# Copying chunk operands to a slot of their own, weighting the head sum in its selector, and keeping a state sum and a gated result in PSUM: a two-layer RWKV-7 and attention kernel

## The chip, the cores and the metric

The kernel runs on one core of a Trainium2 chip. The metric is the device time of one execution in microseconds (us). Before the change it took 797.93 us, the median of three runs (796.20, 797.93, 800.12). The engines are named as the profile names them: PE is the matmul engine and PEld its weight loads, DVE the vector engine, ACT the scalar engine, POOL the third elementwise engine, SP the engine that issues most DMAs. SBUF is the on-chip memory that holds tiles; PSUM is the memory that PE writes to, in 8 banks.

## The reference

The input `x` has 512 tokens of 1024 features. Layer 0 is an RWKV-7 time mixing: four dense projections `r, k, v, g` of the token-shifted input, per-channel decays, and for each of 16 heads of 64 channels a recurrence over the tokens; its output is normalised per head, a bonus is added, and it is gated and projected. Layer 1 is a differential attention. Each layer ends with a per-layer embedding. The lines that the change touches in the kernel compute these:

```python
def step(state, inp):
    r_t, w_t, k_t, v_t, kk_t, a_t = inp
    s_kk = jnp.einsum('bhij,bhj->bhi', state, kk_t)
    state = (state * w_t[:, :, None, :]
             - s_kk[..., None] * (kk_t * a_t)[:, :, None, :]
             + v_t[..., None] * k_t[:, :, None, :])
    return state, jnp.einsum('bhij,bhj->bhi', state, r_t)
...
y = ((y - mean) * lax.rsqrt(var + GN_EPS) * lnx_g.astype(f32).reshape(H, N)
     + lnx_b.astype(f32).reshape(H, N))
y = y + jnp.sum(r * k * r_k.astype(f32), axis=-1, keepdims=True) * v
y = y.reshape(B, S, D).astype(xn.dtype) * jax.nn.silu(g)
return y @ w_out
```

All is float32, with a dense product done as three matmuls of rounded high and low parts (`mm3`, L285 to L287).

## The kernel before

**Staging.** Features lie on the 128 partitions in 8 tiles, tokens along the free axis. From about 85 us the dense projections run, two halves of 512 output features each (half 0 and half 1, `g` in the code below). As the halves of `r, k, v` come out, layer 0 is worked in 8 chunks of 64 tokens for each half: `gram` (L984) builds the products of a chunk pair `cq`; `inverse` (L1013 on), four in all, two for each half, solves the triangular systems of four chunks by 31 substitution steps on DVE (L1051, L1054), then two sets of small matmuls (L1087, L1101), and copies the results back with small copies of 32 x 128 (L270 is the helper `copy`, used with many tiles; L1115). `operands` transposes each chunk's `BK` tile on PE (L1149), `recur` carries the 64 x 64 states of 8 heads through the chunks, and `finish` normalises, adds the bonus, gates, transposes and splits the result in a high and a low part for the output projection. POOL clears tiles (L1144, L1212) and does parts of the finish. Half 0's recurrence lies at about 162 to 243 us, half 1's at 305 to 379; dense matmuls of the other half, of `p` and `g`, and then of the output projection fill PE between the steps.

**One chunk of the recurrence.** Products of the chunk (L1188) and the state's part (L1201) sum up in a bank `pA`; part of it is copied to `gt` (an H tile cleared by POOL at L1212), products with `gt` are added, and a part is copied to `uv`. L1229 multiplies the transposed operands with `uv` into a bank `pS`; DVE adds this to the state (L1241, SBUF plus PSUM, written to SBUF) and multiplies with the chunk's decay `pcall` (L1244, SBUF to SBUF), which the next chunk's L1201 waits for. ACT copies the output to `yT` (L1249).

**What sets the order.** The order of all instructions on each engine, and of the DMAs on SP, is fixed when the program is written: a planner, `Streams`, runs the stages as coroutines. A `yield` of an engine and a cost asks for the next instructions; `wait` and `set` are events; `take` and `free` count buffers: `R` (43 tiles of 128 x 1024), `H` (9 of 128 x 512), PSUM banks (`pw`, `pd`). The planner takes the step that could start first by its own clocks and costs; a `+` behind an engine's name also takes a port that its DVE and POOL steps share, a `!` lets a stage's next step start without waiting for this one; a choice such as `ACT/DVE+` goes to the engine that would be done first. So changed costs, waits or buffers move instructions far from the lines that are edited. On the chip each engine works its own list in order and waits for semaphores.

**Names.** `hsel` is a selector of 128 x 32 that sums the channels of each head on PE (L824); `rkvec` holds the weights `r_k`; `rk` the products r times k. `BK` holds keys by token and feature, `vcD`, `gD`, `mD`, `peD` lie in DRAM, `in_eye` is an input with a unit matrix; L1030 copies it from an H tile to the bank in which DVE substitutes. L1501 copies a product of the `p` embedding out of PSUM. L749 and L750 belong to the decays' small projections, L1456 and L1414 to the output of the layers, and L521 and L525 to the mixing of the input.

Of the kernel before, what the change touches and what calls it, by code (L numbers as in the profile page):

```python
# [8 lines left out]
F32 = mybir.dt.float32  # L9
F32R = mybir.dt.float32r  # L10
AF = mybir.ActivationFunctionType
ALU = mybir.AluOpType
# [190 lines left out]
def yoco_kernel(ctx: ExitStack, tc: tile.TileContext, I, out):  # L203
# [489 lines left out]
    hsel = later("hsel", [P, 32])  # L693
    rkvec = later("rkvec", [P, NT])
    der = T(ax, [P, 6, NT], "der")
    omm = T(ax, [P, 4, NT], "omm")
# [117 lines left out]
    SQ, CK = {}, {}  # L814

    def head_sums(g, what):

# [5 lines left out]
        for q in range(4):  # L823
            nc.tensor.matmul(pn[32 * q : 32 * q + 32], hsel, SQ[what, 4 * g + q], start=True, stop=True)  # L824
        yield "free", "H", 4
# [31 lines left out]
    def k_evac(i, pk):  # L857
# [44 lines left out]
        nc.gpsimd.tensor_mul(v4(rk), part_r(i), K)  # L902
        yield "ACT", 0.57
        nc.scalar.activation(rk, rk, AF.Copy, scale=rkvec[:, i : i + 1])
        yield "set", ("rk", i)
# [15 lines left out]
    sc.add(x_scale(), XLP[0])  # L921
    sc.add(late_loads(), 1)
    for g in range(2):
        sc.add(lora2(g), LO2P[g])
# [196 lines left out]

    def bkt(i, cq, par):
        return BK[i][:, cq, 2 * par : 2 * par + 2, :].rearrange("p a j -> p (a j)")

    def operands(g):
# [4 lines left out]
        for c_ in range(NC):  # L1130
# [4 lines left out]
            if par == 0:  # L1135
                yield "take", "R", 1
                UV[cq, g] = R([P, 2, S])
            t = UV[cq, g][:, par]
# [9 lines left out]
            for ii in range(4):  # L1148
                nc.tensor.transpose(pt[:, ii * P : (ii + 1) * P], bkt(4 * g + ii, cq, par), ident)  # L1149
            yield "ACT", 0.63  # L1150
            for ii in range(4):
                nc.scalar.copy(bkt(4 * g + ii, cq, par), pt[:, ii * P : (ii + 1) * P])
            yield "free", "pw", 1
# [4 lines left out]
    def recur(g):  # L1158
# [14 lines left out]
        for c_ in range(NC):  # L1173
# [49 lines left out]
            if c_ < NC - 1:  # L1223
                yield "take", "pw", 1
                pS = bank("pw")
                yield "PE", 0.55
                for ii, hh in heads:
                    hs = slice(hh * HN, hh * HN + HN)
                    nc.tensor.matmul(  # L1229
                        pS[hs, cols(ii, hh)], bkt(4 * g + ii, cq, par)[:, hs], uv[:, cols(ii, hh)], start=True, stop=True  # L1230
                    )
                pv = pS.rearrange("p (a b) -> p a b", b=P)
            yield "PE!", 0.55
            products(pA, 1, ROFF, uv, False)
            if c_ < NC - 1:
                for hh in range(2):
                    hs = slice(hh * HN, hh * HN + HN)
                    sv, qv = S_[hs, :, hs], pv[hs, :, hs]
                    if c_ > 0:
                        yield "DVE!", 0.42  # L1240
                        nc.vector.tensor_add(sv, sv, qv)  # L1241
                        qv = sv
                    yield "DVE+!", 0.42
                    nc.vector.tensor_mul(sv, qv, bc(pcall[hs, c_, 4 * g : 4 * g + 4].unsqueeze(2), [HN, 4, HN]))  # L1244
# [6 lines left out]
            if par == 1:  # L1251
                yield "free", "R", 3
            yield "set", ("rec", c_, g)
# [3 lines left out]
    def finish(cq, g):  # L1257
# [60 lines left out]
        ENG[sc.eng].tensor_sub(lo, w, hi.bitcast(F32))  # L1318
        yield "free", "R", 1
# [664 lines left out]
```

## Time and profile before

| what | value |
|---|---|
| median of three runs | 797.93 us (796.20 to 800.12) |
| profiled execution | 797.09 us, span 795.3 us |
| PE busy | 756.1 us, 95% |
| DVE busy | 589.8 us, 74% |
| ACT busy | 454.5 us, 57% |
| POOL busy | 201.9 us, 25% |
| mean granted clock of PE | 0.989 |
| HBM read, written | 110.13 MB, 37.75 MB |

The span is the time from the first to the last instruction that the profiler saw; the rest of the execution's time lies around it. In the rows of a view of groups there stand the line, the engine and the operation, the tile written and the tile read, shape and count, then busy time and the mean of one in ns, and the idle time of the engine just ahead of them with what ended it. A row of waits gives total, times and longest. A row of a timeline or of the chain begins with its start and duration.

### The profile page before, as it was taken

How to read it: one execution, taken by the hardware profiler on the slowest of the kernel's cores; microseconds unless marked ns; L12 is line 12 of the kernel's file. 1: busy time of each engine (PE TensorE's matmuls, PEld its weight loads, DVE VectorE, ACT ScalarE, POOL GpSimd, SP SyncE). 2: the span in 40 equal slices, each digit the busy share in tenths (PEclk: the TensorE clock that was granted, in tenths of full speed). 3: DMA queues.
4: the chain of work that ended last, by engine and by line, in shares of the span. 5: the costliest groups of instructions: out<-in, count | busy, mean ns of one | idle time of the engine just before them, and what ended most of it. 6: DMA issues, size and time to landing. Idle time of an engine off the chain costs nothing.

```text
span 795.3 us, 13941 instructions
## 1 busy us (share of the span) xinstructions
PE 756.1 (95%) x5016; PEld 605.1 (76%) x5016; DVE 589.8 (74%) x1360; ACT 454.5 (57%) x1078; POOL 201.9 (25%) x221
## 2 busy tenths in 40 slices
PE   6899999998999899999989999999999999999996
PEld 3576578875777677777778888887888888888884
DVE  2989999976798898998676685446874768835844
ACT  3779745688875446664444564333764566743431
POOL 2416615521451425666010010000000001100000
PEclk9999999998999899999999999999999999999998
DMA  8585669843684687463446444488943523314602
GB/s 325 197 285 196 245 225 290 298 147 105 209 286 171 217 301 258 145 228 105 133 166 247 133 146 135 172 309 226 312 158 92 159 53 121 117 43 159 259 6 106
DMA packets 66677, 148.79 MB, mean 187 GB/s; under 512 B 6576, under 2 KB 27312, under 8 KB 66608
## 3 DMA queue, kind: packets, MB, share of 16 engines
q1 hardware_dynamic: 43824, 112.25, 41.9%
q10 hardware_dynamic: 22784, 35.66, 13.1%
q8 instruction: 39, 0.64, 0.3%
q14 instruction: 30, 0.25, 0.1%
HBM read 110.13 MB, written 37.75 MB: 186 GB/s over the span
## 4 chain that ended last, share of the span: by engine, by line
PE 70%; DVE 8%; ACT 8%; DMA 8%; issue 2%; POOL 2%; SPq 1%; ACTq 0%; POOLq 0%; DVEq 0%
PE p L285 18%; PE p L287 18%; PE p L286 18%; PE p L1788 2%; PE p L984 2%; PE p L1188 2%; ACT R L270 1%; PE p L1753 1%; PE p L1752 1%; PE p L1201 1%; DMA R<-bD 1%; PE p L1779 1%; DMA RAW<-in_ple_w 1%; PE p L1410 1%; DMA R<-mD 1%
## 5 line engine op out<-in xcount | busy, mean ns | idle before, releaser
L285 PE MATMUL p<-R,R 128*128 128x512 f32 x800 | 326.4, 408 | 3.2 <-DVE R L270 1.7
L286 PE MATMUL p<-R,R 128*128 128x512 f32 x800 | 314.1, 393 | 3.8 <-DVE R L525 3.6
L287 PE MATMUL p<-R,R 128*128 128x512 f32 x800 | 314.4, 393 | 0.0
L285 PEld LDWEIGHTS p<-R,R 128*128 128x128 f32 x800 | 151.3, 189 | 37.1 <-DVE R L270 1.9
L287 PEld LDWEIGHTS p<-R,R 128*128 128x128 f32 x800 | 151.0, 189 | 33.2 <-DVE R L1318 0.4
L286 PEld LDWEIGHTS p<-R,R 128*128 128x128 f32 x800 | 151.5, 189 | 32.4 <-DVE R L525 4.9
L318 POOL TENSOR_TENSOR R<-RAW,R 128x512 fp32r<-128x512 f32 x59 | 78.6, 1339 | 163.3 <-ACT R L270 89.1
L270 ACT CAST R<-RAW 128x512 fp32r<-128x512 f32 x110 | 66.1, 619 | 26.7 <-DMA RAW<-in_w_g 10.0
L318 DVE TENSOR_TENSOR R<-RAW,R 128x512 fp32r<-128x512 f32 x81 | 56.8, 715 | 11.0 <-ACT R L270 10.2
L324 DVE SCALAR_TENSOR_TENSOR R<-RAW,vec,R 128x512 fp32r<-128x512 f32 x64 | 46.6, 748 | 13.9 <-ACT R L322 13.7
L322 ACT ACTIVATE R<-RAW,vec 128x512 fp32r<-128x512 f32 x64 | 44.6, 720 | 17.0 <-DMA RAW<-in_b_w_in 9.1
L1397 POOL TENSOR_TENSOR hr<-hm,half 128x1 f32<-128x1 f32 x16 | 10.4, 648 | 147.2 <-DVE hm L1395 147.2
L1757 DVE CUSTOM_DVE_ANT_0 p<-p,cmask 128x128 f32<-128x128 f32 (+3 forms) x64 | 30.3, 509 | 17.4 <-PE p L1753 17.3
L1764 ACT ACTIVATE H<-p,mx 128x128 f32<-128x128 f32 (+3 forms) x64 | 33.3, 526 | 15.7 <-DVE mx L1761 14.1
L281 POOL TENSOR_TENSOR orr<-orm,half 128x4 f32<-128x4 f32 x8 | 8.4, 1055 | 123.3 <-DVE orm L279 93.3
L1054 DVE TENSOR_TENSOR p<-p,H 128x126 f32<-128x126 f32 (+22 forms) x124 | 32.6, 263 | 4.3
L1051 DVE TENSOR_TENSOR H<-p,R 128x126 f32<-128x126 f32 (+22 forms) x124 | 30.5, 246 | 1.1
L1534 DVE SCALAR_TENSOR_TENSOR R<-H,R 128x512 f32<-128x512 f32 x16 | 11.1, 691 | 24.5 <-ACT H L1527 23.1
L1527 ACT ACTIVATE H<-p 128x512 f32<-128x512 f32 x16 | 9.5, 596 | 31.6 <-PE p L287 31.6
L521 DVE SCALAR_TENSOR_TENSOR p<-R,vec,p 128x511 f32<-128x511 f32 x32 | 23.5, 747 | 5.4 <-ACT p L519 5.3
L519 ACT ACTIVATE p<-R,omm 128x512 f32<-128x512 f32 x32 | 22.0, 695 | 5.0 <-DVE R L525 3.7
L1788 PEld LDWEIGHTS p<-R,H 128*128 128x128 f32 x160 | 22.1, 191 | 2.8 <-ACT H L1805 0.5
(227 smaller groups left out, 1249.4 us busy)
## 6 DMA issues: line engine op xcount, KB each, us to landing
R<-mD SPq DMA_DIRECT2D x40, 512.0 KB, 5.3
mD<-R ACTq DMA_DIRECT2D x32, 512.0 KB, 4.3
RAW<-in_ple_gate SPq DMA_DIRECT2D x16, 512.0 KB, 3.7
RAW<-in_kv_w SPq DMA_DIRECT2D x16, 512.0 KB, 3.9
RAW<-in_b_w_in SPq DMA_DIRECT2D x16, 512.0 KB, 3.9
R<-bD ACTq DMA_DIRECT2D x24, 256.0 KB, 5.2
R<-in_x SPq DMA_DIRECT2D x8, 512.0 KB, 6.8
RAW<-in_w_r SPq DMA_DIRECT2D x8, 512.0 KB, 4.0
```

The lines of the kernel that those rows point to most:

```text
L270: (nc.scalar.copy if sc.eng == "ACT" else ENG[sc.eng].tensor_copy)(dst, src)
L285: nc.tensor.matmul(ps, ah, bh, start=first, stop=False)
L286: nc.tensor.matmul(ps, ah, bl, start=False, stop=False)
L287: nc.tensor.matmul(ps, al, bh, start=False, stop=last)
L318: ENG[sc.eng].tensor_sub(lo, f, hi.bitcast(F32))
L322: nc.scalar.activation(hi, f, AF.Copy, scale=g)
L324: nc.vector.scalar_tensor_tensor(lo, f, g, hi.bitcast(F32), ALU.mult, ALU.subtract)
L1051: ve.tensor_mul(tmp[:, 0:m, 0:w], bc(xs[:, s_ : s_ + 1, 0:w], [P, m, w]), bc(nb[:, s_ + 1 : 32, s_ : s_ + 1], [P, m, w]))
L1054: ve.tensor_add(xs[:, s_ + 1 : 32, 0:w], xs[:, s_ + 1 : 32, 0:w], tmp[:, 0:m, 0:w])
L1757: nc.vector.tensor_tensor_reduce(scs[m][:, 0:n], scs[m][:, 0:n], cmask[:, S - n : S], 1.0, -3.0e38, ALU.add, ALU.max, mx[:, m : m + 1])
L1764: nc.scalar.activation(E[m][:, 0:n], scs[m][:, 0:n], AF.Exp, bias=mx[:, m : m + 1], scale=0.125, accum_out=sm[:, m : m + 1])
L1788: nc.tensor.matmul(po[:, x * P : (x + 1) * P], aT[:, kb * P : (kb + 1) * P], vT[hg, kb // 2][:, kb % 2, x * P : (x + 1) * P], start=(kb == 0),
```

## The change

Four edits:

1. **Bonus.** The weights `r_k` are multiplied once into a set of eight selectors `hselr` (one DVE multiply of 128 x 8 x 32, after the first dense half of `r` is out), and the head sum of `rk` uses these. The scaling of each `rk` tile on ACT (L904, eight of 128 x 512) is gone.
2. **Operands.** The four transposes of a chunk were copied from their bank back into the `BK` tiles by four ACT copies of 128 x 128 (L1152); now one ACT copy of 128 x 512 writes them to a new `R` tile `BT`, shared by the chunk pair, from which the state product L1229 reads. A chunk pair takes two `R` tiles where it took one, and frees four where it freed three.
3. **State.** The sum of state and product is written back into the bank (`qv`), and the multiply with the decay reads it from there; the multiply no longer takes the planner's shared port.
4. **Finish.** The gated result (`scalar_tensor_tensor`, L1310) is written back into its bank; ACT always copies the high part from there, DVE always subtracts for the low part, and the bank is freed behind both. Before, the result went to the SBUF tile `w`, the bank was freed at once, and the planner chose ACT or DVE for the copy, POOL or DVE for the subtraction.

```diff
+    hselr = T(ax, [P, NT, 32], "hselr")
...
+    def bonus_maps():
+
+        yield "wait", ("r", 0)
+        yield "DVE+", 0.4
+        nc.vector.tensor_mul(hselr, bc(hsel.unsqueeze(1), [P, NT, 32]), bc(rkvec.unsqueeze(2), [P, NT, 32]))
+
...
-            nc.tensor.matmul(pn[32 * q : 32 * q + 32], hsel, SQ[what, 4 * g + q], start=True, stop=True)
+            sel = hsel if what == "sq" else hselr[:, 4 * g + q, :]
+            nc.tensor.matmul(pn[32 * q : 32 * q + 32], sel, SQ[what, 4 * g + q], start=True, stop=True)
...
-        yield "ACT", 0.57
-        nc.scalar.activation(rk, rk, AF.Copy, scale=rkvec[:, i : i + 1])
...
+    sc.add(bonus_maps(), 5)
...
             if par == 0:
-                yield "take", "R", 1
-                UV[cq, g] = R([P, 2, S])
+                yield "take", "R", 2
+                UV[cq, g], BT[cq, g] = R([P, 2, S]), R([P, 2, S])
...
-            yield "ACT", 0.63
-            for ii in range(4):
-                nc.scalar.copy(bkt(4 * g + ii, cq, par), pt[:, ii * P : (ii + 1) * P])
+                bk = BK[4 * g + ii][:, cq, 2 * par : 2 * par + 2, :].rearrange("p a j -> p (a j)")
+                nc.tensor.transpose(pt[:, ii * P : (ii + 1) * P], bk, ident)
+            yield "ACT", 0.5
+            nc.scalar.copy(BT[cq, g][:, par], pt)
...
-                        pS[hs, cols(ii, hh)], bkt(4 * g + ii, cq, par)[:, hs], uv[:, cols(ii, hh)], start=True, stop=True
+                        pS[hs, cols(ii, hh)], BT[cq, g][:, par, cols(ii, hh)], uv[:, cols(ii, hh)], start=True, stop=True
...
                         yield "DVE!", 0.42
-                        nc.vector.tensor_add(sv, sv, qv)
-                        qv = sv
-                    yield "DVE+!", 0.42
+                        nc.vector.tensor_add(qv, qv, sv)
+                    yield "DVE!", 0.42
                     nc.vector.tensor_mul(sv, qv, bc(pcall[hs, c_, 4 * g : 4 * g + 4].unsqueeze(2), [HN, 4, HN]))
...
-                yield "free", "R", 3
+                yield "free", "R", 4
...
-            nc.vector.scalar_tensor_tensor(w[:, xs], pt[:, xs], vcol(V_LB, 4 * g + x), gt[:, xs], ALU.add, ALU.mult)
-        yield "free", "pw", 1
+            nc.vector.scalar_tensor_tensor(pt[:, xs], pt[:, xs], vcol(V_LB, 4 * g + x), gt[:, xs], ALU.add, ALU.mult)
...
-        yield "ACT/DVE+", (0.52, 0.34)
-        copy(hi, w)
-        yield "Pool+/DVE+", (1.23, 0.6)
-        ENG[sc.eng].tensor_sub(lo, w, hi.bitcast(F32))
+        yield "ACT", 0.48
+        nc.scalar.copy(hi, pt)
+        yield "DVE", 0.6
+        nc.vector.tensor_sub(lo, pt, hi.bitcast(F32))
+        yield "free", "pw", 1
```

Lines of the changed kernel stand 5 to 9 below those of the kernel before: L1115 is L1122 there, L1030 is L1037, L1501 is L1506, L1249 is L1254, L1212 is L1218, L1144 is L1150, L1272, L1274, L1288, L1291 and L1293 are L1277, L1279, L1293, L1296 and L1298.

The planner makes a new order of it. On ACT, at the copies of the second inverse (half 0, 180 to 190 us before), the list was

```order
L1249 COPY R_1732<-p_1829 64x2x128 x2
L780 ACTIVATE H_1863<-p_1939,der_96 128x512
L270 COPY R_1064<-H_1849 32x2x2x32 x4
L270 COPY R_1065<-H_1849 32x2x2x32 x3
L270 COPY R_1205<-H_1849 32x2x2x32 x2
L270 COPY R_1206<-H_1849 32x2x2x32 x2
L1115 COPY R_1064<-p_1987 32x2x2x32
L1115 COPY R_1064<-p_1988 32x2x2x32
L1115 COPY R_1065<-p_1987 32x2x2x32
L1115 COPY R_1065<-p_1988 32x2x2x32
L1115 COPY R_1205<-p_1987 32x2x2x32
```

and is now

```order
L880 COPY H_1978<-p_1470 128x512
L1254 COPY R_1721<-p_1817 64x2x128 x2
L270 COPY R_1063<-H_1838 32x2x2x32 x4
L270 COPY R_1064<-H_1838 32x2x2x32 x4
L270 COPY R_1204<-H_1838 32x2x2x32 x3
L270 COPY H_2020<-p_1989 64x2x128 x2
L270 COPY R_1204<-H_1838 32x2x2x32
L270 COPY R_1205<-H_1838 32x2x2x32 x2
L1122 COPY R_1063<-p_1932 32x2x2x32
L1122 COPY R_1063<-p_1933 32x2x2x32
L1122 COPY R_1064<-p_1932 32x2x2x32
```

The two copies to `gt` (`H_2020`) of a chunk of the recurrence now stand among the inverse's copies to `G` (11 before and 14 now from ACT, then eight L1115 or L1122), and an activation of the decays (L780) no longer stands ahead of them.

On ACT around the copy of `in_eye` for the first inverse of half 1 (258 to 266 us before), the list was

```order
L1501 COPY H_2970<-p_2935 128x512
L1501 COPY H_2983<-p_2969 128x512
L1030 COPY p_3010<-H_2994 128x512
L270 COPY H_2993<-R_2877 32x128 x3
L270 COPY H_2993<-R_2878 32x128 x3
L1501 COPY H_3005<-p_2982 128x512
L1501 COPY H_3042<-p_3004 128x512
```

and is now

```order
L1506 COPY H_2915<-p_2870 128x512
L1506 COPY H_2933<-p_2914 128x512
L1506 COPY H_2961<-p_2932 128x512
L1037 COPY p_2996<-H_2983 128x512
L270 COPY H_2982<-R_2860 32x128 x4
L270 COPY H_2982<-R_2861 32x128 x4
L1506 COPY H_2975<-p_2960 128x512
```

One copy of the `p` embedding behind L1037 remains where two stood behind L1030, and eight small copies of the inverse where six were.

On POOL in the recurrence of half 1 (355 to 375 us before), the end of the list was

```order
L1144 MEMSET R_4250 64x2x128 x2
L1212 MEMSET H_4270 128x512
L1272 TENSOR_TENSOR R_4251<-R_4251,vmean_92 128x512
L281 TENSOR_TENSOR grsr_4240<-grsm_4239,half_90 128x8
L1288 TENSOR_TENSOR R_3485<-R_3485,grsr_4240 128x512
L1144 MEMSET R_4250 64x2x128 x2
L1274 TENSOR_TENSOR R_4251<-R_4251,bon_100 128x512
L1212 MEMSET H_4390 128x512
```

and is now

```order
L1218 MEMSET H_4112 128x512
L1150 MEMSET R_4093 64x2x128 x2
L1277 TENSOR_TENSOR R_4095<-R_4095,vmean_92 128x512
L281 TENSOR_TENSOR grsr_4137<-grsm_4136,half_90 128x8
L1279 TENSOR_TENSOR R_4095<-R_4095,bon_101 128x512
L1296 TENSOR_TENSOR R_3476<-R_3476,R_1704 128x512
L1298 TENSOR_TENSOR R_3476<-R_3476,R_3868 128x512
L1150 MEMSET R_4093 64x2x128 x2
L1218 MEMSET H_4254 128x512
```

Between two clearings of `gt` POOL has five steps of the finish where it had four, beside the operands' memsets. On PE the same recurrence now has 3 to 6 dense matmuls between a chunk's steps, where 9 to 21 stood, and its last product stands 48 dense matmuls earlier; 84 dense matmuls now follow the last finish's transposes before their result is first used, where the use followed at once.

More of the change, by code (lines that the diff above doesn't have):

```diff
@@ L1120, in inverse @@
         yield "set", ("prep", g, cp)
-    def bkt(i, cq, par):
-        return BK[i][:, cq, 2 * par : 2 * par + 2, :].rearrange("p a j -> p (a j)")
+    BT = {}
     def operands(g):
@@ L1148, in operands @@
             for ii in range(4):
-                nc.tensor.transpose(pt[:, ii * P : (ii + 1) * P], bkt(4 * g + ii, cq, par), ident)
-            yield "ACT", 0.63
-            for ii in range(4):
-                nc.scalar.copy(bkt(4 * g + ii, cq, par), pt[:, ii * P : (ii + 1) * P])
+                bk = BK[4 * g + ii][:, cq, 2 * par : 2 * par + 2, :].rearrange("p a j -> p (a j)")
+                nc.tensor.transpose(pt[:, ii * P : (ii + 1) * P], bk, ident)
+            yield "ACT", 0.5
+            nc.scalar.copy(BT[cq, g][:, par], pt)
             yield "free", "pw", 1
```

## The prediction, before the result was known

> **What bounds the kernel now.** I read the page first: the span and the busy time of each engine.
>
> ```profile
> span 795.3 us, 13941 instructions
> PE 756.1 (95%) x5016; PEld 605.1 (76%) x5016; DVE 589.8 (74%) x1360; ACT 454.5 (57%) x1078; POOL 201.9 (25%) x221
> ```
>
> PE is busy for 756.1 of 795.3 us, so a change that takes no matmul away, as this one, can win at most the 39.2 us in which PE stands still, and what PE runs below full clock. The edits lie between about 85 and 400 us. So I next read PE's waits, grouped by who ended them (us in total, times, longest):
>
> ```profile
> PE p L984 <- ACT H L1501: 3.1, 1, 3.1
> PE p L749 <- ACT R L1115: 1.8, 1, 1.8
> PE p L285 <- DVE R L270: 1.7, 1, 1.7
> PE p L1201 <- DVE R L1244: 1.6, 2, 0.8
> PE p L285 <- DVE R L800: 1.4, 1, 1.4
> ```
>
> These five rows, 9.6 us, are what the change can reach; the longer waits of that list belong to the start and the end of the program. Then the stretches, 20 us each (columns: PE, weight loads, DVE, ACT, POOL busy, granted clock, DMA share, GB/s), and two of 10 us:
>
> ```profile
> 180.00:200.00 20.00, 16.36 (x174) 11.93 (x167) 13.01 (x26) 16.19 (x44) 3.86 (x6) 0.83 0.36 122
> 200.00:220.00 20.00, 19.22 (x191) 15.36 (x189) 15.18 (x30) 17.67 (x41) 9.75 (x12) 1.00 0.54 188
> 220.00:240.00 20.00, 19.17 (x246) 15.07 (x245) 19.05 (x36) 13.13 (x33) 10.83 (x15) 1.00 0.88 305
> 340.00:360.00 20.00, 19.16 (x180) 15.37 (x179) 19.10 (x33) 12.28 (x32) 14.08 (x15) 1.00 0.68 224
> 360.00:380.00 20.00, 19.32 (x214) 14.90 (x213) 16.55 (x35) 8.91 (x23) 11.16 (x11) 1.00 0.34 100
> 185.00:195.00 10.00, 7.68 (x64) 5.84 (x65) 6.76 (x12) 9.46 (x23) 2.46 (x2) 0.66 0.14 44
> 262.00:272.00 10.00, 6.88 (x30) 5.34 (x29) 7.80 (x22) 7.61 (x20) 3.76 (x3) 0.66 0.40 136
> ```
>
> Two places stand out. At 185 to 195 ACT is full (9.46 of 10) while PE has 7.68, and the clock is 0.66: 0.34 x 10 = 3.4 us of full speed lost beside the waits. The same loss stands at 262 to 272. Everywhere else from 200 to 380 PE is over 19 of 20 busy, which leaves about 0.8 us per stretch.
>
> **The change part by part.** *Work that goes.* The groups by line:
>
> ```profile
> L904 ACT ACTIVATE H<-H,rkvec 128x512 f32<-128x512 f32 x8 | 5.8, 722 | 0.0
> L1152 ACT COPY R<-p 128x128 f32<-128x128 f32 x64 | 12.2, 278 | 1.9 <-PE p L1149 1.8
> L1456 ACT COPY R<-p 128x512 f32<-128x512 f32 x16 | 9.4, 587 | 24.6 <-PE p L287 24.4
> L1244 DVE TENSOR_TENSOR R<-R,pcall x24: 407/422/1280, 177.6 to 372.0; 64x256 f32<-64x256 f32 x24
> L1244 DVE TENSOR_TENSOR R<-p,pcall x4: 389/422/427, 166.8 to 308.4; 64x256 f32<-64x256 f32 x4
> L1318 DVE TENSOR_TENSOR R<-R,R 128x512 fp32r<-128x512 f32 x8 | 6.4, 796 | 0.4 <-ACT R L270 0.2
> L525 DVE TENSOR_TENSOR R<-p,R 128x512 fp32r<-128x512 f32 x32 | 21.4, 682 | 0.9 <-ACT R L523 0.5
> L521 DVE SCALAR_TENSOR_TENSOR p<-R,vec,p 128x511 f32<-128x511 f32 x32 | 23.5, 747 | 5.4 <-ACT p L519 5.3
> ```
>
> The bonus edit takes 8 scalings off ACT, 5.8 us, and adds one DVE multiply of 128x256 (under 0.69, L525's time for twice the width). The operands' 64 copies, 12.2 us, become 16 of the form of L1456, 9.4: 2.8 us less. Of the eight `hi` copies of the finish, those that DVE did now go to ACT, three at 0.587: 1.8 us more. ACT: 5.8 + 2.8 - 1.8 = 6.8 us less.
>
> On DVE the 24 state multiplies that read two SBUF tiles have a median of 422 ns but up to 1280; the four that read PSUM end at 427. If the tail goes, 15.2 us (24 x 0.633) becomes 24 x 0.422 = 10.1. The `lo` subtraction falls from 796 to L525's 682, 0.9 us for eight. DVE: 6 us less, and its outputs into PSUM (the add, the STT of the finish) I bound by L521, in place in PSUM, 747 against 682 for L525: 0 to 0.065 us for each of 24 adds and 32 STTs, at most 3.6 us. I take 0, since a state add reads PSUM at 422 like the rest.
>
> [...]
>
> Busy time saved on an engine with slack moves the end only where PE waits for it, so I walked the new order at those places.
>
> *Second inverse, 180 to 192.* ACT there, and what PE waited for:
>
> ```profile
> 180.21 3.35 ACT L270 COPY R<-H 32x128 f32<-32x128 f32 x11
> 183.57 2.14 ACT L1115 COPY R<-p 32x128 f32<-32x128 f32 x8
> 185.48 0.50 PE L749 MATMUL p<-R,R 128*128 128x512 f32 x1 [1.81 <-ACT R L1115]
> 187.13 1.12 PE L1188 MATMUL p<-H,R 128*64 128x64 f32 x16 [0.48 <-DVE H L270]
> 189.61 0.79 PE L285 MATMUL p<-R,R 128*128 128x512 f32 x1 [1.35 <-DVE R L800]
> ```
>
> The 19 small copies, 5.5 us, make the jam, and the new order keeps all of them in a row and moves three more from DVE to ACT (0.9); only what stands around them is lighter, and two copies of `gt` are now let in between. Waits of 1.81 + 0.48 + 1.35 = 3.6 become by my walk 0.85 + 1.9, less what the missing L780 and split copies give: I take 2.6, so -1.0. Bounds: 0 (the jam is the same) to -7.0 (3.6 and the clock's 3.4).
>
> *200 to 240.* PE misses 0.78 + 0.83 = 1.6 us there while ACT or DVE is at 17 to 19 of 20; half of L904 lay here. I take -0.5, bounds 0 and -1.6.
>
> *The `eye` copy before the g=1 inverses.*
>
> ```profile
> 258.44 0.38 SPq L1025 DMA_DIRECT2D H<-in_eye  x1
> 263.02 0.59 ACT L1030 COPY p<-H 128x512 f32<-128x512 f32 x1 [4.84 <-DMA H<-in_eye]
> 265.39 1.07 ACT L1501 COPY H<-p 128x512 f32<-128x512 f32 x2
> 266.03 2.08 PE L984 MATMUL p<-R,R 64*128 64x128 f32 x16 [3.12 <-ACT H L1501]
> ```
>
> L1030 holds ACT's queue for 4.84 us until `eye` lands; behind it stands an L1501 copy whose bank the gram L984 needs. The new order puts one L1501 more ahead of L1030, two inverse copies more behind, and the gram still waits for the L1501 that comes last; SP sends `eye` one transfer later. I walk the wait to 2.3 instead of 3.1: -0.8. But PE has 87 matmuls instead of 93 between the last gram and the inverse's products, 6 x 0.23 = 1.4 us less cover for DVE's unchanged substitution, and two more DVE steps (2 x 0.2): net +1.0. Bounds: -6.5 (3.1 and the clock) to +3.
>
> *300 to 310.* The L1201 wait for a stretched L1244, 0.8, goes with the stretch: -0.8; bounds 0 and -1.6.
>
> *Recurrence of g=1.* The new order ends it 48 dense matmuls, 10.9 us, earlier, by putting 3 to 6 dense matmuls between a chunk's steps where 9 to 21 stood. Each step has less to hide its copies behind. One wait of the weight loads for POOL, and the prices of POOL's work and of a dense matmul in the chain:
>
> ```profile
> PEld p L1188 <- POOL H L1212: 0.8, 1, 0.8
> L281 POOL TENSOR_TENSOR grsr<-grsm,half 128x8 f32<-128x8 f32 x8 | 13.2, 1652 | 16.3 <-DVE grsm L279 16.2
> L1272 POOL TENSOR_TENSOR R<-R,vmean 128x512 f32<-128x512 f32 x8 | 9.3, 1167 | 11.5 <-DMA R<-vcD 11.5
> L1274 POOL TENSOR_TENSOR R<-R,bon 128x512 f32<-128x512 f32 x8 | 8.8, 1108 | 0.2
> L1291 POOL TENSOR_TENSOR R<-R,R 128x512 f32<-128x512 f32 x2 | 2.8, 1382 | 0.6 <-DVE R L1288 0.6
> L1293 POOL TENSOR_TENSOR R<-R,R 128x512 f32<-128x512 f32 x3 | 4.4, 1481 | 1.8 <-DVE R L1291 1.7
> L1144 POOL MEMSET R<- 64x256 f32 x32 | 10.2, 322 | 1.7 <-POOL H L1212 0.5
> L1212 POOL MEMSET H<- 128x512 f32 x16 | 8.4, 526 | 7.2 <-DVE R L734 6.0 <-PE p L1087 1.0
> 340.01 0.23 PE p L285
> ```
>
> POOL's clearing of `gt` (L1212) queues behind the finish, and the products L1188 behind it. Between the clearings of `H_4112` and `H_4254` the new order gives POOL four L1144, L1272, L281, L1274, L1291 and L1293: 1.29 + 1.17 + 1.65 + 1.11 + 1.38 + 1.48 + 0.53 for the clearing = 8.6 us. PE has per chunk its products, transposes and some 20 dense matmuls, 20 x 0.23 = 4.6, about 8 in all: POOL is a little behind there. My walk gives 3.5 us of waits (0.9 for a bank behind ACT's inverse copies, 1.1 for a `gt` copy, 1.1 for L1212, 0.4 small) where the old stretch, 20 - 19.16 and 20 - 19.32, has 1.5: I take +1.9. Bounds -1.5 and +5.
>
> *Tail of the layer.* The L285 wait of 1.7 for the last finish is covered: 84 dense matmuls, 19 us, now follow that transpose's place. With the earlier z another 0.5 at the wait for `in_x` behind: -2.2. Bounds 0 and -3.9. The finish holds its bank longer, by one ACT copy and one DVE subtraction (0.59 + 0.68), hidden by those same matmuls; without that cover 1.3 per finish.
>
> Sum: -1.0 - 0.5 + 1.0 - 0.8 + 1.9 - 2.2 = -1.6. The profiled execution took 797.09 (span 795.3 and 1.8 around it), which gives 795.5. The median shown is 797.93, 0.8 above it; I put **796**.
>
> **The rivals.** *Faster: the jam dissolves.* With 6.8 us off ACT and no stretched multiply, the copies at the second inverse come in time for PE, and the clock does not drop: -7.0 instead of -1.0, so 796 - 6 = **790**. For it: ACT's 9.46 of 10 there. Against: the nineteen small copies stay, and the drop to 0.66 came with no gap over 1.81 us, so halving the gaps need not end it. [...]
>
> *Slower: POOL paces the recurrence of g=1.* If three more chunks wait for L1212 as the one in my walk does, 3 x 1.03, the term is +5 instead of +1.9; and if the gaps gather as at 185, one more drop of 3.4 comes on top: 796 + 3.1 + 3.4 = **802.5**. For it: 8.6 against 8. It decides from the point where POOL has over 8 us between two clearings in four of the seven later chunks. Against: the old order once gave POOL 8.6 too (the same rows, two L1293, three L1144 and no L1272), and PE's only wait for a clearing is the 0.8, though more dense matmuls lay between.
>
> *The stretch is not the port's.* If L1244 stays at 633 ns reading PSUM, and the PSUM outputs cost their 0.065, DVE is no lighter: -0.8 goes, the rest stands: **797**.
>
> **How the numbers follow.** Chances: forecast 0.42, jam dissolves 0.30, POOL paces 0.20, no stretch removed 0.08. A run cannot tell less than 0.5%, 4 us, from no change: faster means under 794, slower over 802. Faster: 0.28 from the first rival and 0.06 from the forecast's low edge, 0.34. Slower: 0.17 and 0.05 of the forecast's high edge, 0.22. Same: 0.44. The range takes in 790 and 802.5, and a little beyond each: 789 to 803; the forecast alone is 793 to 799.
>
> **What would show it.** L1244 with no multiply over 0.45 us, and the 128x512 operand copy at 0.59: right on costs. The window 185 to 195 with clock 1.00: the first rival. A wait of L1188 for POOL's L1212 of more than 2 us in all, or a clock under 1.00 in 300 to 380: the second. The L285 wait for the last finish gone: the tail term. Wrong altogether if a new wait over 3 us stands at a place not listed, such as a bank held by the finish, or in the attention after 420 us, which I take as unchanged.

## The result and the profile after

The changed kernel took 806.38 us, the median of three runs (804.79 to 807.14), against 797.93. The ratio on record is 1.0126 of the time before, with a 95% interval of 1.0093 to 1.0159; the two medians alone give 1.0106. It is slower, by a little over 1%. In a later set of runs, beside runs of the kernel before at 794.17, it gave 1.0111 (1.0083 to 1.0140). The profiled execution took 806.38, its span 804.6, so 9.3 us more span than before.

The page after, its busy time and its clock in 40 slices:

```profile
span 804.6 us, 13893 instructions
PE 758.7 (94%) x5016; PEld 608.4 (76%) x5016; DVE 584.5 (73%) x1339; ACT 454.2 (56%) x1039; POOL 206.3 (26%) x226
PEclk9999999999999888999999999999999999999998
```

PE has the same 5016 matmuls and is busy 2.6 us longer; it stands still for 804.6 - 758.7 = 45.9 us instead of 39.2. So 6.7 of the 9.3 us are waits; the other 2.6 stand beside a lower mean clock (0.982 against 0.989). DVE is 5.3 us less busy than before, and the time went up.

The stretches after (columns as before):

```profile
180.00:200.00 20.00, 17.60 (x200) 12.98 (x198) 13.05 (x27) 18.82 (x46) 3.11 (x7) 1.00 0.35 119
200.00:220.00 20.00, 18.06 (x170) 13.61 (x169) 17.34 (x27) 14.37 (x30) 12.70 (x15) 1.00 0.58 192
220.00:240.00 20.00, 18.03 (x206) 13.80 (x202) 16.15 (x31) 13.64 (x28) 9.17 (x10) 0.92 0.78 279
260.00:280.00 20.00, 16.16 (x81) 12.70 (x80) 15.55 (x47) 9.55 (x25) 8.60 (x7) 0.83 0.54 183
280.00:300.00 20.00, 15.95 (x124) 13.13 (x123) 19.00 (x67) 6.15 (x12) 5.79 (x5) 0.87 0.82 299
300.00:320.00 20.00, 16.58 (x170) 12.37 (x170) 16.38 (x37) 9.13 (x26) 9.38 (x11) 0.78 0.72 243
320.00:340.00 20.00, 16.86 (x309) 13.98 (x310) 15.56 (x27) 14.93 (x43) 13.90 (x15) 1.00 0.28 93
380.00:400.00 20.00, 19.80 (x115) 16.00 (x111) 14.51 (x30) 8.86 (x19) 5.03 (x4) 1.00 0.51 165
400.00:420.00 20.00, 19.59 (x92) 15.97 (x90) 10.71 (x18) 9.39 (x21) 1.11 (x2) 1.00 0.53 185
```

Three of these places before, in stretches of 40 us:

```profile
260.00:300.00 40.00, 35.27 (x269) 28.49 (x270) 35.20 (x116) 20.23 (x51) 15.54 (x13) 0.91 0.72 254
300.00:340.00 40.00, 39.21 (x518) 31.10 (x517) 37.58 (x78) 26.14 (x73) 25.09 (x27) 1.00 0.62 209
380.00:420.00 40.00, 36.13 (x170) 28.96 (x168) 28.45 (x55) 17.76 (x39) 4.60 (x5) 1.00 0.49 161
```

PE's idle time by stage, before and after, is the length of the stretch minus PE's busy time: 180 to 260 from 5.3 to 6.8 us (+1.5); 260 to 300 from 4.7 to 7.9 (+3.2); 300 to 340 from 0.8 to 6.6 (+5.8); 380 to 420 from 3.9 to 0.6 (-3.3). The clock is at 0.92 or less in four stretches (220 to 240 and 260 to 320); before it was so in two (180 to 200 and 260 to 280). The longest waits of PE after, and behind them the wait at the inverse's products as it was before:

```profile
PE p L1094 <- DVE H L1082: 4.1, 1, 4.1
PE p L1194 <- ACT H L270: 4.0, 4, 2.0
PE p L991 <- ACT H L1506: 3.8, 1, 3.8
PE p L1194 <- DVE H L270: 3.4, 1, 3.4
```

```profile
PE p L1087 <- DVE H L1075: 1.6, 1, 1.6
```

L1094 and L991 are the inverse's products and the gram of half 1 (L1087 and L984 before); L1194 is the recurrence's products (L1188 before). What the edits were to do to single instructions stands in these rows:

```profile
L1249 DVE TENSOR_TENSOR R<-p,pcall x28: 415/422/428, 166.0 to 376.7; 64x256 f32<-64x256 f32 x28
L1158 ACT COPY R<-p x16: 567/586/608, 131.9 to 370.7; 128x512 f32<-128x512 f32 x16
L1322 DVE TENSOR_TENSOR R<-p,R x8: 677/691/692, 337.7 to 394.5; 128x512 fp32r<-128x512 f32 x8
L1315 DVE SCALAR_TENSOR_TENSOR p<-p,vec,R x32: 352/359/360, 334.2 to 393.5; 128x128 f32<-128x128 f32 x32
L1086 DVE TENSOR_TENSOR H<-H,unit x4: 673/762/4514, 148.4 to 319.2; 128x512 f32<-128x512 f32 x4
```

No state multiply is over 428 ns now, the operand copy takes 586, the subtraction 691. One result written into PSUM takes 359 ns where it took a mean of 341, but it costs more than that. The four of a step overlapped before (the first row; they began 0.26 us apart) and do not now (the second; 0.39 apart):

```profile
327.17 1.11 DVE L1310 SCALAR_TENSOR_TENSOR R<-p,vec,R 128x128 f32<-128x128 f32 x4
```

```profile
334.20 1.54 DVE L1315 SCALAR_TENSOR_TENSOR p<-p,vec,R 128x128 f32<-128x128 f32 x4 [1.26 <-PE p L1309]
```

For the eight steps that is 8 x 0.43 = 3.4 us of DVE's time. And L1086, an instruction that the change does not touch, once takes 4514 ns where its middle is 762.

### The profile page after: what moved, and what is told of

Same layout as the page of the kernel before. It is cut to its first block, busy times and chain, and to the rows that moved or that the text cites. A ratio compares the mean times of both kernels' runs of the same rounds, so it can differ in the third digit from the quotient of the medians.

```text
span 804.6 us, 13893 instructions
## 1 busy us (share of the span) xinstructions
PE 758.7 (94%) x5016; PEld 608.4 (76%) x5016; DVE 584.5 (73%) x1339; ACT 454.2 (56%) x1039; POOL 206.3 (26%) x226
## 4 chain that ended last, share of the span: by engine, by line
PE 66%; DVE 11%; ACT 9%; DMA 8%; issue 3%; POOL 1%; SPq 0%; ACTq 0%; DVEq 0%; POOLq 0%
PE p L285 17%; PE p L287 17%; PE p L286 17%; PE p L1793 2%; ACT R L270 2%; PE p L991 2%; DMA R<-mD 1%; PE p L1194 1%; PE p L1758 1%; DMA H<-in_eye 1%; PE p L1757 1%; DMA RAW<-in_ple_w 1%; PE p L1784 1%; DMA R<-bD 1%; DMA gD<-H 1%
## 5 line engine op out<-in xcount | busy, mean ns | idle before, releaser
L285 PE MATMUL p<-R,R 128*128 128x512 f32 x800 | 327.1, 409 | 0.1
L285 PEld LDWEIGHTS p<-R,R 128*128 128x128 f32 x800 | 151.3, 189 | 33.8 <-issue 1.9
L318 POOL TENSOR_TENSOR R<-RAW,R 128x512 fp32r<-128x512 f32 x62 | 83.0, 1347 | 159.8 <-ACT R L270 77.2
L270 ACT CAST R<-RAW 128x512 fp32r<-128x512 f32 x107 | 64.4, 618 | 27.8 <-DMA RAW<-in_w_k 8.0
L318 DVE TENSOR_TENSOR R<-RAW,R 128x512 fp32r<-128x512 f32 x78 | 54.5, 709 | 18.1 <-ACT R L270 17.5
L1402 POOL TENSOR_TENSOR hr<-hm,half 128x1 f32<-128x1 f32 x16 | 10.4, 648 | 152.6 <-DVE hm L1400 152.6
L1061 DVE TENSOR_TENSOR p<-p,H 128x126 f32<-128x126 f32 (+17 forms) x124 | 32.6, 263 | 4.3
L1058 DVE TENSOR_TENSOR H<-p,R 128x126 f32<-128x126 f32 (+17 forms) x124 | 30.6, 247 | 1.1
L1461 ACT COPY R<-p 128x512 f32<-128x512 f32 x16 | 9.4, 589 | 29.5 <-PE p L287 29.5
L991 PE MATMUL p<-R,R 64*128 64x128 f32 x256 | 20.9, 304 | 4.3 <-ACT H L1506 3.8
L991 PEld LDWEIGHTS p<-R,R 64*128 64x128 f32 x256 | 17.4, 204 | 9.6 <-ACT H L1506 4.3
```

Of the source, the lines that this page charges most:

```text
L270: (nc.scalar.copy if sc.eng == "ACT" else ENG[sc.eng].tensor_copy)(dst, src)
L285: nc.tensor.matmul(ps, ah, bh, start=first, stop=False)
L318: ENG[sc.eng].tensor_sub(lo, f, hi.bitcast(F32))
L991: nc.tensor.matmul(pg[hh][:, x : x + P], BK[i][hs, cq, 2 * par : 2 * par + 2, :], AR[i][hs, cq, 2 * par : 2 * par + 2, :], start=True, sto ...
L1058: ve.tensor_mul(tmp[:, 0:m, 0:w], bc(xs[:, s_ : s_ + 1, 0:w], [P, m, w]), bc(nb[:, s_ + 1 : 32, s_ : s_ + 1], [P, m, w]))
L1061: ve.tensor_add(xs[:, s_ + 1 : 32, 0:w], xs[:, s_ + 1 : 32, 0:w], tmp[:, 0:m, 0:w])
```

## The experiments

In the first two parts the order of the instructions is held and single things are altered; in the last each edit is planned anew. Theory A is that the edited instructions are harmless and the loss is in the new order. Theory B is that the edited instructions cost the time. Each group of runs had its own runs of the kernel before (medians 793.9 to 794.5 us); ratios are to those.

### The edits in the old order, and the old instructions in the new order

`h13_old_order` has before's order, row for row, with two edits as instructions: the planner's requests stay as they were.

```diff
+    def bonus_maps():
+        yield "wait", ("r", 0)
+        nc.vector.tensor_mul(hselr, ...)
...
         yield "ACT", 0.57
-        nc.scalar.activation(rk, rk, AF.Copy, scale=rkvec[:, i : i + 1])
...
-                        nc.vector.tensor_add(sv, sv, qv)
-                        qv = sv
+                        nc.vector.tensor_add(qv, qv, sv)
                     yield "DVE+!", 0.42
```

> The order of before, row for row, with the instructions of two edits in it: the bonus weights in the selector (eight ACT scalings gone, one DVE multiply added) and the state sum in PSUM. Theory A, the loss comes from the new order and not from the edited instructions: 794 to 798 us, no state multiply over 0.45 us, the two waits of PE for the state multiply (0.8 each) gone or under 0.3. Theory B, the edited instructions themselves cost the time (outputs into PSUM, banks held longer): 800 us or more.

It took 792.73 us: 0.9977 (0.9959 to 0.9994), 1.8 us less than before and somewhat below the 794 to 798 expected. Its multiply and two stretches:

```profile
L1250 DVE TENSOR_TENSOR R<-p,pcall x28: 384/422/429, 167.9 to 369.8; 64x256 f32<-64x256 f32 x28
300.00:320.00 20.00, 20.00 (x332) 15.82 (x332) 17.44 (x39) 11.89 (x34) 12.75 (x15) 1.00 0.81 277
320.00:340.00 20.00, 20.00 (x192) 16.01 (x191) 18.25 (x38) 13.52 (x37) 12.85 (x14) 1.00 0.47 164
```

PE is busy for the whole of 300 to 340; both waits for the state multiply are gone. So these two edits are a small gain where the order stays. The other two could not be held so: the operands' edit needs R tiles that the old plan gives to others, and the finish's edit frees its bank later. What their instructions cost apart from their order, the 3.4 us of the finish among it, is therefore not shown.

`a_state_in_sbuf` is the reverse: the new order with the old state instructions.

```diff
                         yield "DVE!", 0.42
-                        nc.vector.tensor_add(qv, qv, sv)
+                        nc.vector.tensor_add(sv, sv, qv)
+                        qv = sv
                     yield "DVE!", 0.42
```

> The order of the changed kernel, with the state sum and the multiply on SBUF tiles as before. Theory A (the order): 805 to 809 us, the multiply up to 1.3 us again, all waits over 3 us still there. Theory B (the instructions): 3 us or more below the changed kernel's 806.4.

1.0105 (1.0082 to 1.0128), not to be told from the changed kernel's 1.0111, though the multiply is up to 1332 ns again. Its 803.05 us lie below the 805 to 809 expected, as the kernel before lies lower in these runs too. Theory B falls for the state edit: putting the old instructions back saves no 3 us. The loss stays with the new order.

### What the new order runs into

In the changed kernel DVE and POOL at 305 and 319 (start, duration):

```profile
305.78 4.04 DVE L270 COPY R<-H 32x128 f32<-32x128 f32 x4
319.24 4.51 DVE L1086 TENSOR_TENSOR H<-H,unit 128x512 f32<-128x512 f32 x1
```

```profile
305.83 1.32 POOL L318 TENSOR_TENSOR R<-RAW,R 128x512 fp32r<-128x512 f32 x1 [11.49 <-DVE R L270]
307.11 1.04 POOL L1277 TENSOR_TENSOR R<-R,vmean 128x512 f32<-128x512 f32 x1
308.23 1.04 POOL L1279 TENSOR_TENSOR R<-R,bon 128x512 f32<-128x512 f32 x1
319.16 2.04 POOL L1279 TENSOR_TENSOR R<-R,bon 128x512 f32<-128x512 f32 x2
321.16 2.04 POOL L1277 TENSOR_TENSOR R<-R,vmean 128x512 f32<-128x512 f32 x2
```

L1086 starts 0.08 us behind the first of four POOL instructions and ends at 323.75, 0.55 after the last of them: its 4.51 us are 3.83 more than its usual 0.68, nearly the whole train of 4.04. The four small copies, of which one alone takes 0.20, ran beside the other train: the last three (1.22, 0.98 and 1.58 us) each ended 0.08 us behind the end of a POOL instruction, so they went in one by one. PE's wait of 3.4 us, up to 313.26, is for a copy to `gt` which comes behind these copies by way of a transposition on DVE and two steps on ACT; no wait of PE from 300 to 340 names L1086, and what its 4.51 us cost by themselves is not shown.

`a_copies_on_act` takes these DVE instructions away from the meeting; the unit matrix is not subtracted in the second inverse of half 1.

```diff
-        ENG[sc.eng].tensor_sub(xm, x32, bc(unit.unsqueeze(1), [P, 16, 32]))
+        if n == 3:
+            nc.scalar.copy(xm, x32)
+        else:
+            ENG[sc.eng].tensor_sub(xm, x32, bc(unit.unsqueeze(1), [P, 16, 32]))
...
-                    copy(lower(q, u, hh)[...], four(xm[quads[q], sl]))
+                    (nc.scalar.copy if n == 2 else copy)(lower(q, u, hh)[...], four(xm[quads[q], sl]))
```

> The order of the changed kernel, but the inverse's small SBUF copies that DVE does in the first inverse of half 1 (4 taking 4.04 us at 305.8), and the subtraction of the unit matrix in the second (4.51 us at 319.2), are issued on ACT. The subtraction is left out there, a plain copy stands for it. Theory A says these DVE instructions stood still for a train of POOL operations: PE's wait of 3.4 us for the gt copy at 313 falls under 1, and with the clock 799 to 803 us. Theory B, or a theory that DVE was merely busy: 805 to 807 us.

1.0065 (1.0043 to 1.0088), 800.79 us: 3.7 us below the changed kernel by the two ratios (0.0046 x 794). PE's wait of 3.4 for the `gt` copy fell to 1.6, not under 1. The intervals of this run and of the changed kernel (1.0083 to 1.0140) overlap a little, and so they do in the next run and in `a_no_eye_load`: each of these single gains is about as large as its noise.

That could still be 1.5 us of work taken off DVE. `a_pool_without_reads` leaves DVE all its work and changes only what POOL does beside it: the steps of half 0's finish become memsets of the same tile, which read nothing. The bonus of half 0 is left out.

```diff
-        nc.gpsimd.tensor_add(wg, wg, bc(vmean[...].unsqueeze(2), [P, 8, HN]))
+        if g == 0:
+            nc.gpsimd.memset(w, 0.0)
+            nc.gpsimd.memset(w, 0.0)
+        else:
+            nc.gpsimd.tensor_add(wg, wg, bc(vmean[...].unsqueeze(2), [P, 8, HN]))
```

and so for the multiply with the bonus.

> The changed kernel's order and engines, but the eight POOL steps of half 0's finish (mean added, bonus multiplied) are each two POOL memsets of the same tile, about as long, which read nothing: the bonus of half 0 is left out. DVE keeps all its work. If the two long DVE instructions (four copies 4.04 us at 305.8, the subtraction 4.51 at 319.2) stand still because POOL reads SBUF beside them: the subtraction falls to 0.7, the copies to at most 2.2 (the weight split on POOL still reads), and 4 to 7 us go, to 1.003 to 1.007 of before. If DVE is merely loaded or waits for POOL's results: no change, 1.009 to 1.013.

1.0068 (1.0041 to 1.0094), 3.4 us below the changed kernel; the copies take 2.59 us, not the 2.2 at most that were expected. DVE:

```profile
303.48 2.59 DVE L270 COPY R<-H 32x128 f32<-32x128 f32 x4
313.33 0.69 DVE L1086 TENSOR_TENSOR H<-H,unit 128x512 f32<-128x512 f32 x1
315.27 0.69 DVE L1304 TENSOR_TENSOR R<-R,R 128x512 f32<-128x512 f32 x1
317.67 0.68 DVE L1306 TENSOR_TENSOR R<-R,R 128x512 f32<-128x512 f32 x1
```

and POOL beside the last two:

```profile
315.41 0.52 POOL L1284 MEMSET R<- 128x512 f32 x1
317.50 0.52 POOL L1278 MEMSET R<- 128x512 f32 x1
```

The copies still meet the weight split L318, which reads, and take 1.45 us less. Two of them ran beside memsets and were held as well, for about the length of one memset, 0.53 us and this:

```profile
305.49 0.58 DVE L270 COPY R<-H 32x128 f32<-32x128 f32 x1
```

L1086 comes ahead of the train this time, since all before it is earlier. Two instructions with two SBUF inputs, L1304 and L1306, do run into the train, now one of memsets from 314.33 to 318.60, and take their usual 0.69 and 0.68. So of instructions of one shape with two SBUF inputs the one beside POOL's reads was held (L1086 in the changed kernel, 4.51 us) and the ones beside POOL's memsets were not (L1304 and L1306 here), though POOL worked without a break there too. The small copies were held beside both: 1.22 us beside a weight split of 1.32 in the changed kernel, 0.58 beside a memset of 0.53 here. Taking the reads away is worth about 3.4 us.

The second place is the unit matrix. In the changed kernel ACT and DVE around it:

```profile
265.08 0.59 ACT L1037 COPY p<-H 128x512 f32<-128x512 f32 x1 [5.02 <-DMA H<-in_eye]
265.60 2.44 ACT L270 COPY H<-R 32x128 f32<-32x128 f32 x8
268.06 0.59 ACT L1506 COPY H<-p 128x512 f32<-128x512 f32 x1
268.68 1.66 ACT L270 CAST R<-RAW 128x512 fp32r<-128x512 f32 x3
269.85 1.34 DVE L318 TENSOR_TENSOR R<-RAW,R 128x512 fp32r<-128x512 f32 x1 [3.69 <-ACT R L270]
```

ACT waits about as long as before (4.84), but the matrix lands 2 us later and eight copies stand behind it instead of six, so the cast that DVE needs comes late and DVE, which sets the end of the inverse, stands still for 3.69 us (1.82 before).

`a_eye_on_act_queue` sends the matrix from ACT's DMA queue.

```diff
-        nc.sync.dma_start(xs, I["eye32"])
+        nc.scalar.dma_start(xs, I["eye32"])
```

> The changed kernel with the unit matrix of the inverses sent from ACT's DMA queue instead of SP's. If the landing of that matrix (6.63 us behind weight loads) sets the waits at the first inverse of half 1: ACT waits under 2.5 us for it instead of 5.0, PE's wait of 3.8 us falls under 1.5, the clock stays at 1.00 in 262 to 272, and the wait of 4.1 at the inverse's products shrinks by 2 or more: 798 to 801 us. If other work sets them: 805 us or more.

1.0148 (1.0107 to 1.0189): no gain, and no answer. The issue stood behind the L1506 copies in ACT's own order, went out at 261.1 instead of 258.4, and ACT waited 5.05 us all the same.

`a_no_eye_load` needs no DMA: ACT fills the bank with zeros and writes the diagonal from a small table.

```diff
-        nc.sync.dma_start(xs, I["eye32"])
...
-            nc.scalar.copy(xs, eye)
+            nc.scalar.activation(pe, bc(half[:, 0:1], [P, S]), AF.Copy, scale=0.0)
+            nc.scalar.copy(diagonal(pe), bc(dupm.unsqueeze(1), [P, 16, 2]))
```

> The changed kernel's order, but the unit matrix of each inverse is written into its bank by two ACT instructions (a zero fill from a constant, and its diagonal from a 128x2 table), so no DMA is waited for. If the wait for that DMA sets the two waits of PE at the first inverse of half 1 (3.8 and 4.1 us): the first falls under 0.5, the second under 2, and the clock stays above 0.95 in 260 to 300; 6 to 9 us below the changed kernel. If the waits come from the order of the dense work alone: less than 2 us.

1.0074 (1.0049 to 1.0099), against 1.0111 of the changed kernel beside it:

> The changed kernel again, on the chip of this comparison, for its distance to the variants beside it: 1.0126 of before, within its interval of 1.0093 to 1.0159.

That is 2.9 us by the ratios, under the 6 to 9 expected. The wait of L991 is gone, the one at the inverse is not:

```profile
PE p L1104 <- DVE H L1092: 4.4, 1, 4.4
```

DVE is busy for 18.96 of 20 us from 280 to 300 there; PE has simply run ahead of the substitution. So I read the two waits of 3.8 and 4.1 as one debt: DVE's chain, of which the landing of the matrix costs about 3.5 (7.9 less 4.4) of waiting.

`a_no_eye_copies_act` joins this with `a_copies_on_act`; the unit matrix is not subtracted in the second inverse of half 1.

> The one before, together with the small copies and the subtraction on ACT (the subtraction replaced by a plain copy, so the unit matrix isn't subtracted). Theory A: both mechanisms add up, 10 to 14 us below the changed kernel and at or below the kernel before, since the tail of the layer is shorter in this order. If they overlap: no better than the better one of the two.

792.85 us, 0.9975 (0.9959 to 0.9991): 10.8 us below the changed kernel by the ratios, more than the two gains apart (2.9 and 3.7). PE in 300 to 320 goes from 16.58 busy at clock 0.78 to

```profile
300.00:320.00 20.00, 19.94 (x333) 15.69 (x331) 13.80 (x27) 13.83 (x39) 18.11 (x18) 1.00 0.57 189
```

With both gone the new order is no slower than the kernel before. Why the two together give some 4 us more than the sum of the single gains is not shown.

`new_order_mended` gives a whole output: as that one, but the subtraction of the second inverse is done on POOL instead of being left out.

```diff
-            nc.scalar.copy(xm, x32)
+            nc.gpsimd.tensor_sub(xm, x32, bc(unit.unsqueeze(1), [P, 16, 32]))
```

> The changed kernel's order, the unit matrix written by ACT, the first inverse's copies on ACT, and the second's subtraction done on POOL instead of DVE; the output is whole. By theory A as fast as the variant with the plain copy: 0.995 to 1.000 of before.

793.62 us, 0.9999 (0.9981 to 1.0018): level with the kernel before, 8.9 us below the changed kernel by the ratios. `old_order_no_eye_load` is the old order with the bonus and state edits and without the matrix's load:

> The order of before with the bonus and state edits, and the unit matrix written by ACT. By theory A the wait of 3.3 for the matrix and the clock's loss beside it go: 4 to 8 us below the same kernel with the load, so 0.988 to 0.993 of before.

792.96 us, 0.9970 (0.9949 to 0.9991), less than was expected: the 3.3 us wait goes and the one for the substitution rises from 1.8 to 4.1, as in the new order. This and `h13_old_order` beat both kernels; they can't be told apart. So the old order gains next to nothing without the load (0.9970 for 0.9977) where the new one gains 2.9 us: the load is a loss of the new order, and not a gain that any order would have had. For the copies and the subtraction that comparison is missing, since they were not taken off DVE in the old order.

### Each edit planned anew

Is one edit's plan to blame (theory C)? The edits were run alone, each with the diff that the change has for it.

> The kernel before with the bonus edit alone, planned anew. Theory A (a new order falls well or badly by where DVE meets POOL's reads and where the unit matrix lands): no term of its own; it lies where its order's waits between 260 and 345 put it, 0.995 to 1.010. Theory C (one edit's plan brings the loss): 0.995 to 1.000 unless it is this one, then 1.008 or more.

> The kernel before with the finish edit alone (result and split in PSUM), planned anew; its order is the nearest to the one before. Theory A: 0.996 to 1.004. Theory C: 1.008 or more if this edit brings the loss, by the bank held longer.

> The kernel before with the operands' edit alone, planned anew. Theory C (the bonus edit's plan is the one that loses): 0.996 to 1.003. Theory A (any new plan can): up to 1.010, and if over 1.005, with the same signature between 260 and 345: DVE instructions over 2 us long beside POOL's reads, or a wait over 3.5 us at the inverse's products.

> The kernel before with the state edit alone, planned anew. With the order held, this edit and the bonus edit gave 0.9977. Theory C: 0.995 to 1.001. Theory A: anywhere from 0.993 to 1.010, by the same signature.

> The changed kernel without the bonus edit (the scalings are back on ACT), planned anew. Theory C: the loss goes, 0.995 to 1.002 of before. Theory A: no rule; if the signature between 260 and 345 is there it is 1.006 or more, else 0.995 to 1.003.

| edits, planned anew | of before | interval | longest waits of PE, 180 to 410 us |
|---|---|---|---|
| bonus | 1.0123 | 1.0099 to 1.0147 | L1094 4.1, L991 3.0, L1195 2.5 |
| finish | 1.0030 | 1.0012 to 1.0049 | L984 3.2, L285 2.3 |
| operands | 1.0116 | 1.0085 to 1.0148 | L1087 6.8, L1303 2.8 |
| state | 1.0082 | 1.0049 to 1.0115 | L1188 4.5, L984 3.0 |
| all but bonus | 1.0117 | 1.0083 to 1.0152 | L1087 5.2, L1187 3.5 |
| all four | 1.0111 | 1.0083 to 1.0140 | L1194 4.1, L1094 4.1, L991 2.6 |

Theory C falls: the loss does not belong to one edit, and does not add up. The finish edit, whose order is nearest to the old one, costs least; each plan that moves much loses 0.8 to 1.2%, each with long waits of its own. With the state edit alone the longest hold of DVE lies elsewhere, at a subtraction of the finish (the first row is DVE's, then POOL's):

```profile
340.99 5.14 DVE L1317 TENSOR_TENSOR R<-R,R 128x512 fp32r<-128x512 f32 x1
```

```profile
340.30 1.27 POOL L1292 TENSOR_TENSOR R<-R,R 128x512 f32<-128x512 f32 x1
341.52 1.04 POOL L1273 TENSOR_TENSOR R<-R,bon 128x512 f32<-128x512 f32 x1
342.53 2.04 POOL L1271 TENSOR_TENSOR R<-R,vmean 128x512 f32<-128x512 f32 x2
344.53 1.04 POOL L1273 TENSOR_TENSOR R<-R,bon 128x512 f32<-128x512 f32 x1
345.51 0.67 POOL L1144 MEMSET R<- 64x256 f32 x2
```

L1317, which takes 0.69 us at other places of that run, ends at 346.13, 0.56 behind POOL's last read and after POOL comes to its memsets at 345.51. But the two places of the changed kernel do not explain every plan. With the operands' edit alone one DVE instruction between 260 and 345 is held by more than 1 us, L1292 at 318.98, which takes 2.38 us. With all but the bonus none is held by more than 0.9. In neither does ACT wait for the matrix at its copy; it waits for DVE there (3.10 and 1.86 us). Their longest waits, 6.8 and 5.2, are PE's for the inverse's chain on DVE, which is busy for 18.83 and 18.75 of 20 us from 280 to 300. A wait of 4.1 to 4.8 at that place stands in `new_order_mended` and `old_order_no_eye_load` too, which lose nothing, so what makes these two plans slow is open. Why the old plan escapes nearly all of this is not settled. That its priorities were found for this very order would explain it; it was not tried.

## Why the prediction was wrong

The forecast was 796 us in a range of 789 to 803, likeliest no change that can be told; 806.38 lies 3.4 above the range. In the later set of runs the kernel before was at 794.2 and the changed one at 803.4. The step that failed is the recurrence of half 1, with the `eye` term beside it; the other terms come first.

*Work that goes: right on the copies and the multiplies, wrong on the outputs into PSUM.* The multiply's tail is gone (428 ns at most for 1280), 5.1 us in all, and the subtraction gives 0.9, as foreseen. The outputs into PSUM were taken at 0; the results now keep DVE busy for 11.5 us instead of 8.9 and the sums for 10.4 instead of 10.0, 3.0 us together, near the upper bound of 3.6. That DVE is 5.3 us less busy for the 6 foreseen is luck: against the saving stand these 3.0 and the 3.8 by which L1086 is held, and for it work that the plan gave to other engines (1339 instructions for 1360). The held-order run shows what the bonus and state edits are worth, 1.8 us. ACT's 6.8 us less do not show in its sum (454.2 for 454.5), since the new plan gave it 14 more instructions than the edits leave it (1039, where 1078 - 48 - 8 + 3 = 1025); I booked only the edits.

*Second inverse, -1.0: right on the waits, too small in all.* PE idles 2.4 us in 180 to 200 instead of 3.6, and the clock stays at 1.00, also from 185 to 195. That was the first rival's sign, and with it came the 3.4 us of clock that the term left out; the kernel was slower all the same. *200 to 240, -0.5: wrong.* Idle time rose from 1.6 to 3.9 us: waits of 2.0 for a `gt` copy behind POOL's clearing and a weight split, 1.2 at L901 for a copy by ACT and 0.7 at L1156, that I had not walked; the clock fell to 0.92 in 220 to 240.

*`eye`, +1.0: too small.* The waits rose from 4.7 to 7.9, +3.2, just over the upper bound of +3, with the clock at 0.87 behind them. My list of five waits had left out the 1.6 at L1087, which stands in the same list and grew to 4.1. I took the wait of the gram to shrink to 2.3; it was 3.8 and 2.6 in two profiles. The point missed is who is late: I counted PE's cover and two DVE steps, not that DVE itself stands idle behind ACT's held queue (3.69).

*Recurrence of half 1, +1.9, and 300 to 310, -0.8: the step that failed.* Together they should have cost 1.1 us; 300 to 340 cost 5.8 of waits and a clock of 0.78 in its first half. Of its 6.6 us of idle time 3.4 are the wait for DVE's held copies; the other 3.1 are three waits for copies on ACT. And 340 to 380, where the term's wait was read, cost nothing (1.6 us of idle time for 1.5; the walk's 3.5 less 1.5 is also 2.0, not 1.9). I looked for a stretch at L1244 alone, where the old trace showed it (up to 1280 ns for 422), and gave every other DVE instruction its usual time. The old rows held the warning: in the trace before, of these five small copies one took 0.23 us, and the other four, from 319.57 on, took 3.23 beside a POOL train, at a place where PE did not wait for them:

```profile
319.32 3.48 DVE L270 COPY R<-H 32x128 f32<-32x128 f32 x5
```

With L1244 and these copies two kinds of DVE instruction were held beside POOL in that trace, so the new order had to be read for where POOL's trains lie beside DVE's work.

*Tail, -2.2: right in sign and size,* -3.3 by the windows, within its bounds.

*The rivals.* The slower one had the right sign and engine but in the main the wrong mechanism: it let POOL's clearing of `gt` be late in half 1. Both its signs came, a clock under 1.00 after 300 and a wait for the clearing of more than 2 us, by the weight loads:

```profile
PEld p L1194 <- POOL H L1218: 2.4, 1, 2.4
```

But that wait stands at 236.86, in the recurrence of half 0, and is one with the 2.0 of above. In half 1 the longest wait comes by another way: POOL delays DVE (four copies in 4.04 us), and DVE delays PE (3.4). The third, that the stretch stays, did not come for L1244; the stretch moved to other instructions, which no rival said. The chance of 0.22 for slower was too low in this sense: all that the prediction summed were the places where the old order had waits, and a plan made anew opens others.

## What to carry to other kernels

Where a planner makes the order, an edit is two changes, its instructions and a new plan; run the edit with the old order held to see what it is worth, and the new plan apart. Before a new plan is trusted, list the trains of POOL's SBUF reads and which of DVE's instructions lie beside them (here L1086 took 4.51 us for 0.68), in the whole stage and not only where the old trace showed a stretch. Look at what stands behind a wait for a small load: here ACT waited 5.02 us for the unit matrix, and behind it, by way of a cast, DVE for 3.69.

## What the runs showed of the hardware

DVE instructions with two SBUF inputs were shut out by a whole train of POOL instructions that read: L1086 of the changed kernel stood through four in a row (4.51 us for 0.68) and ended 0.55 us behind the last; L1317 of the state edit alone stood through five (5.14 for 0.69) and ended 0.56 behind the last. Beside memsets alone L1304 of `a_pool_without_reads` took 0.69. It was not always so. In the changed kernel L318 on DVE, which began at 269.85 and took 1.34 us (this line's mean is 0.71), was done at 271.19, before the second of these two reads of POOL had ended:

```profile
269.37 2.96 POOL L318 TENSOR_TENSOR R<-RAW,R 128x512 fp32r<-128x512 f32 x2 [5.23 <-ACT R L270]
```

What decides whether it gets in is not settled. The small copies went in between two instructions of POOL, one at a time (1.22, 0.98 and 1.58 us for 0.20), and were held beside memsets too (0.53 and 0.58).

A DVE result written into PSUM in place took a mean of 358 against 341 ns for 128x128, and 432 against 416 for the state sum. Four of the 128x128 results in a row took 1.54 us instead of 1.11: they began 0.39 us apart instead of 0.26.

The granted clock fell by other amounts from run to run of one kernel. In the first profile of the changed kernel it was 0.83, 0.87 and 0.78 in the three stretches from 260 to 320, where PE stood idle for 3.8, 4.1 and 3.4 us, and its page has 8 tenths in the three slices from 261 to 322; the page of `after_again` has 9, 9 and 8 there:

```profile
PEclk9999999999999998999999999999999999999999
```

Which wait it takes is not settled.
